# The head of a decoder layer: activation tiles and the first weight chunk taken token tile by token tile

## The chip, the cores and the metric

One core of one Trainium2 chip. TensorE (PE) multiplies, VectorE (DVE) and ScalarE (ACT) do the elementwise work, GpSimd (POOL) a few small operations, and SyncE (SP) issues the loads. The metric is the device time of one execution in microseconds (us). Before the change it is 766.53 us, the median of three runs (766.51 to 766.59).

## The reference, cut to what matters

```python
mod = silu(c) @ w_mod + b_mod                       # c: (1, 1024), w_mod: (1024, 6*1024)
sh_m, sc_m, gt_m, sh_f, sc_f, gt_f = split(mod, 6)
h = rms_norm(x, g_mix_norm) * (1.0 + sc_m) + sh_m    # x: (512, 1024)
proj = h @ w_in                                      # (512, 5704): queries, keys, values, gates
...                                                  # two sparse attentions, gates, w_out
x = x + gt_m * (merged @ w_out)
h = rms_norm(x, g_ffn_norm) * (1.0 + sc_f) + sh_f
x = x + gt_f * ((silu(h @ w_gate) * (h @ w_up)) @ w_down)
```

Everything is float32. The change touches only the first two hundred instructions or so: the normalization of x, the part of the modulation that it needs, and the first 128 of the 1024 rows of `w_in`.

## The kernel before, in words

**Tiles.** Tokens come in four tiles of 128 (`NT`), features in eight chunks of 128 (`NK`). x is loaded as four token tiles into two buffers `xa` (tag O); an x tile is 512 KB. A matmul needs features on partitions, so each x tile is transposed block by block on TensorE (`turn`, a product with `identr`) after it was scaled by 1/rms. The transposed x is kept in `xnT` (tag O): two buffers of four chunks each.

**Scale of a token.** For tile i: ACT squares it and sums the row (`V<-O` in the profile), DVE adds EPS (`m<-ssx`), POOL raises to -0.5 (`m<-m,mhalf`), DVE multiplies the tile (`O<-O,m`).

**Modulation of a chunk.** For chunk k the kernel needs the 128 scales and 128 shifts of its features: a product of silu(c) with a strip of `w_mod` (tag K, two loads of 512 KB: m=1 for the scale, m=0 for the shift). It sums eight blocks j per half: ACT does the first two (`first_products`, `gu<-K,cs`), DVE adds some of the others (`add_up`, `gu<-K,cs,gu`, then `gu<-gu`), and for chunks 0 and 1 TensorE takes the blocks named in `direct` (`pstr<-cs,K`). A product with a column of ones (`pstr<-one,gu`) sums DVE's part over the partitions. The two columns that come out are called `pc`. From them come the columns `acol` and `mcol`, and the normalized chunk is `x*acol+mcol`.

**High and low parts.** A float32 product is made of three fast ones: each operand is split into a rounded high part and the rest. For the activations these are `hh` and `hl` (tag H; `s` holds the unrounded chunk, and DVE subtracts, `H<-s,H`), for the weights `wh` (an ACT cast of the loaded `st`) and `wl` (a DVE subtraction, `wl<-st,wh`).

**The first group.** `first_group(k, ...)` multiplies chunk k's four token tiles with 512 columns of keys (banks `acc_k`, tag psacc) and three of them with 512 columns of index queries (banks `acc_q` in the banks pspv, pss, pstr): seven outputs, three products each, 21 matmuls. In the middle of group k-1 stands `between`, the `pc` products of chunk k. The loop over k runs `add_up(k+1)`, group k-1 with chunk k's `pc`, then `shift_scale(k)` (`acol`, `mcol` on ACT), `high`, `s`, `low`, and the weights of chunk k+1.

**Order.** Each engine runs its own instructions in the order in which the code issues them; the head is written out by hand. Behind the head a planner in the kernel places small tasks between the matmuls by costs of its own. PSUM has four banks psacc, two pstr, one pspv, one pss. `unused_products` are matmuls whose result nobody reads. All loads of the head go through SP's queue, in order; before they are x 0 to 3, strip 0, first weights 0, strip 1, first weights 1.

Instructions of PE, DVE, ACT and POOL go through a recording wrapper, so the profile gives them all the wrapper's line, L111; they are told apart by their tiles.

Of the kernel before, what the change touches and what calls it, by code (L numbers as in the profile page):

```python
# [23 lines left out]
F32 = mybir.dt.float32  # L24
# [93 lines left out]
def layer(ctx, tc, x, vecs, w_mod, w_in, gvecs, w_br_dsa, w_br_moba, w_out, w_gate_up, w_down, cosh, sinh, cosi, sini, out):  # L118
# [102 lines left out]
    for i in range(NT):  # L221
        nc.sync.dma_start(xa[i // 2][:, i % 2, :], xv[:, i, :])
    strips = [load_strip(0)]
    firsts = [load_first(0)]
    strips.append(load_strip(1))
    firsts.append(load_first(1))

# [31 lines left out]
    def first_group(k, wh, wl, between):  # L259
# [4 lines left out]
        def high_high(n0, n1):  # L264
            for acc, i, ws in outs[n0:n1]:
                te.matmul(acc, hh[:, sls[i]], wh[:, 0, ws], start=k == 0, stop=False)
# [9 lines left out]
        if not k:  # L276

            high_high(0, 4)
            high_low(0, 4)
            high_high(4, 7)  # L280
            low_high(0, 4)
            high_low(4, 7)
            between()
            low_high(4, 7)
            return
# [7 lines left out]
    with tc.manual_schedule(engines=engines):  # L293
# [16 lines left out]
        direct = {(0, 1): (5, 6, 7), (0, 0): (5, 6, 7), (1, 1): (6, 7), (1, 0): (6, 7)}  # L310
# [51 lines left out]
        def turn(i, ks):  # L362
            for k in ks:
                te.transpose(xps[k][:, i * P:(i + 1) * P], xa[i // 2][:, i % 2, k * P:(k + 1) * P], ident)

        def unused_products(n, where=None):

            where = bank[:, 1:] if where is None else where[:, P:]
            for _ in range(n):
                te.matmul(where, identr, identr.unsqueeze(1).to_broadcast([P, 3, P]), start=True, stop=True)  # L370

        def keep(k, eng):
            eng(xnT[k // 4][:, k % 4, :], xps[k])


        xps = [ps(g) for g in ["tr", "pv", "s"] + ["acc"] * 4]
        bank = ps("tr", (P, 4, P))
        pc = bank[:, 0, 0:2]
        ws = []
        xs = [xa[i // 2][:, i % 2, :] for i in range(NT)]  # L380
        rs = [small([P, 1]) for _ in range(NT)]

# [3 lines left out]
        def rstd(i, more):  # L386
            ve.tensor_scalar(rs[i], ssx[:, i:i + 1], more, None, op0=ALU.add)
            ge.tensor_tensor(out=rs[i], in0=rs[i], in1=mhalf[:, 0:1], op=ALU.pow)

        unused_products(14)  # L390
        for i in range(NT - 1):
            se.activation(junk, xs[i], AF.Square, scale=D ** -0.5, accum_out=ssx[:, i:i + 1])
            rstd(i, EPS)
            if i < NT - 2:
# [47 lines left out]
        for k in range(1, NK):  # L442
# [6 lines left out]
            if k == 1:  # L449
                first_products(2)  # L450
# [1520 lines left out]
```

## Time and profile before

| | |
|---|---|
| median of three runs | 766.53 us (766.51 to 766.59) |
| span of the profiled execution | 764.9 us; what lies around it, against the median, is 1.6 us |
| TensorE | busy 756.1 us, 99% of the span |
| VectorE, ScalarE, GpSimd | busy 603.4, 413.6 and 62.1 us |
| granted TensorE clock | 1.000 over the span |
| loads and stores | 137.10 MB, 179 GB/s on average |

The profile page gives the span, not a time of its own for the profiled execution; so the span is set against the median. Rows of the timeline give start and duration in us, the engine, what is written and read, how many instructions were merged (x4), and in brackets an idle time before them with what ended it. PE's matmuls overlap: the step from one start to the next, not the duration, is what one costs in a row.

### The profile page before, as it was taken

The numbers are of one execution on the slowest core, as the hardware profiler recorded it, in microseconds if no ns is written. First come the engines' busy times: TensorE is split into PE (matmuls) and PEld (weight loads), VectorE is DVE, ScalarE is ACT, GpSimd is POOL, SyncE is SP. The second block draws the span as 40 slices with busy tenths as digits, with TensorE's granted clock in tenths as the row PEclk, the third lists the DMA queues.
The fourth block names the chain that finished last, engine by engine and source line by source line (L and its number), as shares of the span: only waits on it lengthen the run. The fifth ranks groups of instructions, "written<-read, shape, count | busy, mean of one in ns | idle before, by whom it ended". The sixth has DMA issues, their size and how long they took to land.

```text
span 764.9 us, 10986 instructions
## 1 busy us (share of the span) xinstructions
PE 756.1 (99%) x3884; PEld 639.2 (84%) x3884; DVE 603.4 (79%) x1183; ACT 413.6 (54%) x888; POOL 62.1 (8%) x91
## 2 busy tenths in 40 slices
PE   7999999999999999999999999999999999999998
PEld 6887888888788887888888988889999998888886
DVE  6974889989799796336867897878788856997897
ACT  6763786879868666643534443543444432554431
POOL 2000012011111000000000000000011020012100
PEclk9999999999999999999999999999999999999999
DMA  9976252542125455533440146744565679589982
GB/s 324 353 212 227 85 169 81 159 129 59 40 79 198 134 147 179 175 98 131 143 152 1 56 150 205 243 153 133 182 204 186 198 254 377 185 264 390 311 324 82
DMA packets 87921, 137.10 MB, mean 179 GB/s; under 512 B 9008, under 2 KB 49272, under 8 KB 87228
## 3 DMA queue, kind: packets, MB, share of 16 engines
q1 hardware_dynamic: 79992, 105.71, 43.5%
q0 software_dynamic: 7792, 30.67, 11.2%
q8 instruction: 30, 0.49, 0.3%
q14 instruction: 23, 0.19, 0.1%
q10 hardware_dynamic: 84, 0.04, 0.0%
HBM read 117.52 MB, written 18.88 MB: 178 GB/s over the span
## 4 chain that ended last, share of the span: by engine, by line
PE 97%; DVE 1%; ACT 0%; DMA 0%; issue 0%; POOL 0%; ACTq 0%
PE psacc L111 62%; PE pstr L111 12%; PE pspv L111 11%; PE pss L111 11%; DVE V L111 1%; DVE s L111 1%; DMA pT<-in_vecs_dram 0%; POOL m L111 0%; DVE O L111 0%; ACT H L111 0%; ACT V L111 0%; DVE m L111 0%; ACT acol L111 0%; DVE cols L111 0%; DVE mcol L111 0%
## 5 line engine op out<-in xcount | busy, mean ns | idle before, releaser
L111 DVE TENSOR_TENSOR wl<-st,wh 128x1024 fp32r<-128x1024 f32 (+1 forms) x98 | 113.7, 1160 | 42.3 <-ACT wh L111 32.9
L111 PE MATMUL psacc<-wh,H 128*128 128x512 f32 x384 | 126.4, 400 | 0.5 <-ACT H L111 0.5
L111 ACT CAST wh<-st 128x1024 fp32r<-128x1024 f32 (+1 forms) x98 | 97.7, 999 | 53.2 <-DMA st<-in_w_gate_up_dram 20.7
L111 PE MATMUL psacc<-H,wh 128*128 128x512 f32 x384 | 124.1, 404 | 0.0
L111 PEld LDWEIGHTS psacc<-wh,H 128*128 128x128 f32 x384 | 72.0, 188 | 16.0 <-ACT H L111 1.1
L111 PEld LDWEIGHTS psacc<-H,wh 128*128 128x128 f32 x384 | 70.0, 188 | 15.3 <-issue 2.7
L111 PE MATMUL psacc<-H,wl 128*128 128x512 f32 x192 | 75.1, 391 | 0.0
L111 PE MATMUL psacc<-H,O 128*128 128x256 f32 (+1 forms) x465 | 72.3, 296 | 0.0
L111 PE MATMUL psacc<-wl,H 128*128 128x512 f32 x192 | 71.0, 390 | 0.0
L111 PEld LDWEIGHTS psacc<-H,O 128*128 128x128 f32 x465 | 64.0, 191 | 2.7
L111 POOL TENSOR_TENSOR m<-m,mhalf 128x4 f32<-128x4 f32 (+1 forms) x24 | 28.6, 1192 | 390.1 <-DVE m L111 356.1
L111 PE MATMUL psacc<-K,O 128*128 128x256 f32 x288 | 43.4, 283 | 0.0
L111 PEld LDWEIGHTS psacc<-H,wl 128*128 128x128 f32 x192 | 36.0, 188 | 8.0
L111 PEld LDWEIGHTS psacc<-wl,H 128*128 128x128 f32 x192 | 36.2, 188 | 6.8
L111 PE MATMUL pss<-H,wh 128*128 128x512 f32 x128 | 39.5, 390 | 0.0
L111 PE MATMUL pspv<-H,wh 128*128 128x512 f32 x128 | 39.4, 389 | 0.0
L111 PE MATMUL psacc<-O,wh 128*128 128x512 f32 x128 | 39.4, 389 | 0.0
L111 PEld LDWEIGHTS psacc<-K,O 128*128 128x128 f32 x288 | 38.4, 191 | 0.0
L111 ACT ACTIVATE s<-s,att 128x256 f32<-128x256 f32 (+3 forms) x64 | 34.2, 562 | 4.5 <-DVE att L111 4.3
L111 ACT CAST H<-st 128x512 fp32r<-128x512 f32 (+1 forms) x21 | 16.1, 766 | 23.4 <-PE psacc L111 18.4
L111 ACT CAST O<-pT 128x512 fp32r<-128x512 f32 x24 | 14.7, 621 | 25.7 <-DVE pT L111 25.2
L111 PEld LDWEIGHTS pspv<-H,wh 128*128 128x128 f32 x128 | 24.0, 188 | 5.0
(338 smaller groups left out, 1629.5 us busy)
## 6 DMA issues: line engine op xcount, KB each, us to landing
st<-in_w_in_dram SPq DMA_DIRECT2D x36, 512.0 KB, 3.5
K<-in_w_mod_dram SPq DMA_DIRECT2D x12, 1024.0 KB, 6.5
st<-in_w_gate_up_dram SPq DMA_DIRECT2D x24, 512.0 KB, 4.1
st<-in_w_down_dram SPq DMA_DIRECT2D x22, 512.0 KB, 4.9
st<-in_w_gate_up_dram SPq DMA_DIRECT2D x40, 256.0 KB, 3.6
K<-in_w_mod_dram SPq DMA_DIRECT2D x16, 512.0 KB, 6.3
O<-second POOLq DMA_DIRECT2D x6, 768.0 KB, 8.0
st<-in_w_in_dram SPq DMA_DIRECT2D x16, 256.0 KB, 4.2
```

Of the source, the lines that this page charges most:

```text
L111: inst = f(*args, **kw)
```

## The change

**Loads.** The first strip goes between the x tiles 1 and 2, and the two halves of the first weights go behind x 2 and x 3. Strips and first weights up to strip 3 are issued right behind them; before, they came later in the code but in the same place of SP's queue. On SP before (K is a strip, O an x tile, st first weights):

```order
L222 DMA O_74<-in_x_dram 128x1024 x2
L222 DMA O_75<-in_x_dram 128x1024 x2
L213 DMA K_80<-in_w_mod_dram 128x8x128 x2
L184 DMA st_83<-in_w_in_dram 128x512 x2
L213 DMA K_86<-in_w_mod_dram 128x8x128 x2
L184 DMA st_89<-in_w_in_dram 128x512 x2
```

and now:

```order
L223 DMA O_74<-in_x_dram 128x1024 x2
L213 DMA K_78<-in_w_mod_dram 128x8x128 x2
L223 DMA O_75<-in_x_dram 128x1024
L230 DMA st_first<-in_w_in_dram 128x512
L223 DMA O_75<-in_x_dram 128x1024
L232 DMA st_first<-in_w_in_dram 128x512
L213 DMA K_86<-in_w_mod_dram 128x8x128 x2
L184 DMA st_89<-in_w_in_dram 128x512 x2
```

From K_86 on the queue is as it was; the second pair of x tiles (O_75) moved behind the strip.

**Transposes.** An x tile's eight blocks go into two banks of the tile's own, four chunks each, rather than into one bank per chunk; each bank is then copied to `xnT` by one instruction. Before, chunk 7 was transposed later, inside the loop; now all eight are done in the head.

**Chunk 0, tile by tile.** `first_group` no longer handles chunk 0. Its `pc` is made after x tiles 0 and 1, its products run for tiles 0 and 1 before tiles 2 and 3 are scaled and transposed, and the `pc` of chunk 1 stands among the last of them. TensorE before, from chunk 0's `pc` to the middle of its group:

```order
L111 MATMUL pstr_137<-one,gu_208 128x1
L111 MATMUL pstr_137<-cs,K_80 128x1 x3
L111 MATMUL pstr_137<-one,gu_208 128x1
L111 MATMUL psacc_133<-identr 128x384 x5
L111 MATMUL psacc_249<-wh_218,H_104 128x512
```

and now, from the same place to the transposes of tile 3 and the first query products:

```order
L111 MATMUL psacc_220<-wh_213,H_113 128x512
L111 MATMUL psacc_221<-wh_213,H_113 128x512
L111 MATMUL psacc_220<-wl_214,H_113 128x512
L111 MATMUL psacc_221<-wl_214,H_113 128x512
L111 MATMUL pspv_234<-identr,O_75 128x128 x4
L111 MATMUL pss_239<-identr,O_75 128x128 x4
L111 MATMUL psacc_220<-wh_213,H_115 128x512
L111 MATMUL psacc_221<-wh_213,H_115 128x512
L111 MATMUL psacc_222<-wh_213,H_113 128x512
L111 MATMUL psacc_222<-wl_214,H_113 128x512
L111 MATMUL pstr_254<-identr,O_75 128x128 x4
L111 MATMUL pstr_259<-identr,O_75 128x128 x4
```

Sixteen transposes (those of x tiles 2 and 3, O_75) moved from before chunk 0's products to between them.

**VectorE.** The scaling of x tiles 2 and 3 moved behind chunk 0's columns. Now, from these columns to the low part of the last two tiles:

```order
L111 TENSOR_SCALAR mcol<-pstr_139,cols 128x1
L111 TENSOR_SCALAR H_113<-O_137,acol,mcol 128x256
L111 TENSOR_SCALAR m_1_23_142<-ssx 128x1
L111 TENSOR_TENSOR wl_214<-st_first,wh_213 128x512
L111 TENSOR_SCALAR O_75<-O_75,m_1_23_142 128x1024
L111 TENSOR_SCALAR s_219<-O_137,acol,mcol 128x256
L111 TENSOR_TENSOR H_115<-s_219,H_113 128x256
L111 TENSOR_SCALAR m_1_24_143<-ssx 128x1
L111 TENSOR_SCALAR O_75<-O_75,m_1_24_143 128x1024
```

Both scalings (the rows O_75<-O_75) had been done before the sums of chunk 0. The sums of chunk 2 moved too. Before, with gu_256 and gu_283 the sums of chunks 1 and 2, and H_106 the low part of chunk 1:

```order
L111 TENSOR_TENSOR gu_256<-gu_256 128x256
L111 TENSOR_TENSOR wl_265<-st_89,wh_264 128x1024
L111 SCALAR_TENSOR_TENSOR gu_283<-K_268,cs,gu_283 128x256 x6
L111 TENSOR_TENSOR gu_283<-gu_283 128x256
L111 TENSOR_TENSOR H_106<-s_328,H_104 128x512
```

and now, with gu_283 and gu_319 the sums of chunks 1 and 2, and H_115 the low part of chunk 1:

```order
L111 TENSOR_TENSOR gu_283<-gu_283 128x256
L111 TENSOR_TENSOR wl_303<-st_89,wh_302 128x1024
L111 TENSOR_TENSOR H_115<-s_314,H_113 128x512
L111 SCALAR_TENSOR_TENSOR gu_319<-K_92,cs,gu_319 128x256 x6
L111 TENSOR_TENSOR gu_319<-gu_319 128x256
```

The low part of chunk 1 now stands ahead of the sums of chunk 2. From the weights of chunk 2 on, the order on every engine is what it was.

The diff, cut:

```diff
-    for i in range(NT):
-        nc.sync.dma_start(...)
...
+    load_x(0)
+    load_x(1)
     strips = [load_strip(0)]
-    firsts = [load_first(0)]
+    load_x(2)
+    firsts = [wp.tile([P, 1, 512 + N_Q], F32, name="st_first", tag="st")]
+    nc.sync.dma_start(firsts[0][:, 0, 0:512], w_in[0:P, C_KB:C_KB + 512])
+    load_x(3)
+    nc.sync.dma_start(firsts[0][:, 0, 512:512 + N_Q], w_in[0:P, C_QI:C_QI + N_Q])
...
-        direct = {(0, 1): (5, 6, 7), (0, 0): (5, 6, 7), (1, 1): (6, 7), (1, 0): (6, 7)}
+        direct = {(0, 1): (4, 5, 6, 7), (0, 0): (4, 5, 6, 7), (1, 1): (6, 7), (1, 0): (6, 7)}
...
-        unused_products(14)
+        unused_products(10)
...
+        turn(0, ("pv", "s"))
+        unused_products(1)
+        first_products(0, 1)
+        scale(1)
+        keep(0, 0, se.copy)
+        sum_direct(0, pc, 1)
+        add_up(0, 1)
+        turn(1, ("tr", "acc"))
...
+        sum_up(0, pc, (0,), begun=True)
+        keep(0, 1, se.copy)
+        keep(1, 0, ve.tensor_copy)
+        unused_products(3)
+        square(2)
...
+        scale(2)
+        low_tokens(slice(0, 256))
+        rstd(3)
+        turn(2, ("pv", "s"))
...
+        high_tokens(3)
+        keep(2, 1, se.copy)
...
             if k == 1:
-                first_products(2)
-            if k + 1 < NK:
-                add_up(k + 1)
...
+                first_products(2)
+                add_up(2)
             if k + 1 < NK:
                 next(weights_hi(k + 1))
                 weights_lo(k + 1)
```

In the new code `unused_products` writes into `bank`, the PSUM tile that also holds chunk 0's `pc`; before, the five products behind that `pc` wrote into another bank. The squares of x tiles 2 and 3 are both done whole by ACT (before, DVE took half of the last one).

More of the change, by code (lines that the diff above doesn't have):

```diff
@@ L360, in weights_lo, with turned, keep, unused_products @@
                              op=ALU.subtract)
[L362 to L368, printed above, removed]
+        def turned(i, half, tag):
+            to = ps(tag, (P, 4, P))
+            for q in range(4):
+                k = half * 4 + q
+                te.transpose(to[:, q, :], xa[i // 2][:, i % 2, k * P:(k + 1) * P], ident)
+            return to
+        def keep(i, half, eng):
+            eng(xnT[half][:, :, i * P:(i + 1) * P], turns[i][half])
+        def unused_products(n):
             for _ in range(n):
[L370 to L376, printed above, removed]
+                te.matmul(bank[:, 1:], identr, identr.unsqueeze(1).to_broadcast([P, 3, P]), start=True, stop=True)
         bank = ps("tr", (P, 4, P))
@@ new lines, in product, with shifted, low_tokens @@
+        def product(i, to, part, act, weight, first=False, last=False):
+            te.matmul(to[i], act[:, sls[i]], ws[0][weight][:, 0, part], start=first, stop=last)
+        def shifted(to, src):
+            ve.tensor_scalar(to, src, acol[:, 0, 0:1], mcol[:, 0:1], op0=ALU.mult, op1=ALU.add)
+        def low_tokens(c):
+            shifted(hf0[:, c], xnT[0][:, 0, c])
+            ve.tensor_tensor(out=hl0[:, c], in0=hf0[:, c], in1=hh0[:, c].bitcast(F32), op=ALU.subtract)
+        hh0, hl0 = hk(0)
@@ L420, in layer @@
         ve.tensor_scalar(mcol[:, 0:1], pc[:, 0:1], bm[:, 0:1], None, op0=ALU.add)
+        parts = weights_hi(0, (KB, QI))
         next(parts)
[L422 to L431 removed]
@@ new lines, in layer, with high_tokens @@
+        rstd(3)
+        turn(2, ("pv", "s"))
+        next(parts)
+        for i in range(2):
+            product(i, acc_k, KB, hl0, 0)
+        def high_tokens(i):
+            se.activation(hh0[:, sls[i]], turns[i][0][:, 0, :], AF.Identity, bias=mcol[:, 0:1], scale=acol[:, 0, 0:1])
+        high_tokens(2)
+        keep(2, 0, se.copy)
+        scale(3)
+        product(2, acc_k, KB, hh0, 0, first=True)
+        product(2, acc_k, KB, hh0, 1)
+        keep(1, 1, se.copy)
+        weights_lo(0, QI)
@@ L465, in layer @@
             if k == 1:
-                keep(NK - 1, se.copy)
+                first_products(2)
+                add_up(2)
             if k + 1 < NK:
```

126 lines of the change are left out of this document (67 added, 59 removed).

## The prediction, before the changed kernel was run

> **What bounds the kernel now.** I read first what TensorE waited for over the whole span, then the busy time in four stretches.
>
> ```profile
> PE pstr L111 <- DMA pT<-in_vecs_dram: 4.0, 1, 4.0
> PE pstr L111 <- DVE O L111: 0.5, 1, 0.5
> PE psacc L111 <- ACT H L111: 0.5, 2, 0.3
> ...
> 0.00:15.71 15.71, 10.82 (x69) 9.97 (x69) 8.71 (x28) 9.88 (x20) 4.66 (x12) 1.00 0.91 316
> 15.71:22.76 7.05, 6.86 (x37) 5.62 (x37) 6.98 (x15) 5.41 (x12) 0.00 (x0) 1.00 1.12 363
> 22.76:28.20 5.44, 5.44 (x25) 4.50 (x26) 5.09 (x12) 4.60 (x9) 0.00 (x0) 1.00 1.12 358
> 28.20:764.90 736.70, 732.94 (x3755) 619.10 (x3753) 582.62 (x1133) 393.65 (x850) 57.42 (x79) 1.00 0.53 173
> ```
>
> The first three rows (waiter, what ended the wait, us in all, times, longest) are all the waits that TensorE has, and they lie in the head. In the stretches the columns behind the length are busy time of PE, weight loads, DVE, ACT and POOL. Chunk 0's products begin at 15.71, group 1 at 22.76, group 2 at 28.20, and from there PE works without a wait. So the order behind the head being the same, a shift of group 2's start should reach the end whole, and nothing downstream can take it up. In 15.71:22.76 VectorE is busy 6.98 of 7.05 us: the head is full on two engines, and that is where the change adds and moves work.
>
> TensorE's rows there:
>
> ```profile
> 4.14 3.96 PE L111 MATMUL pstr<-identr 128*128 128x384 f32 x14
> ...
> 11.35 0.60 PE L111 MATMUL psacc<-identr,O 128*128 128x128 f32 x4
> 11.79 0.73 PE L111 MATMUL pstr<-cs,K 128*128 128x1 f32 x6
> 12.38 0.64 PE L111 MATMUL psacc<-identr,O 128*128 128x128 f32 x4
> ...
> 14.26 1.13 PE L111 MATMUL psacc<-identr 128*128 128x384 f32 x5
> 15.71 1.19 PE L111 MATMUL psacc<-wh,H 128*128 128x512 f32 x4 [0.32 <-ACT H L111]
> 16.74 1.08 PE L111 MATMUL psacc<-wl,H 128*128 128x512 f32 x4
> 17.66 0.39 PE L111 MATMUL pspv<-wh,H 128*128 128x512 f32 x1
> ...
> 22.76 1.21 PE L111 MATMUL psacc<-wh,H 128*128 128x512 f32 x4 [0.19 <-ACT H L111]
> ...
> 25.66 0.50 PE L111 MATMUL pstr<-one,gu 128*128 128x1 f32 x4
> ...
> 28.20 1.07 PE L111 MATMUL psacc<-wh,H 128*128 128x512 f32 x4
> ```
>
> Steps from them: a transpose 0.11 (four from 11.35 to 11.79), a direct strip product 0.20 (three, recorded as six, from 11.79 to 12.38), a product of 512 columns 0.23 (four from 16.74 to 17.66), an unused one about 0.2. The product with ones is taken at 0.2 like a direct one.
>
> VectorE's, ScalarE's and GpSimd's:
>
> ```profile
> 6.82 0.75 DVE L111 TENSOR_SCALAR O<-O,m 128x1024 f32<-128x1024 f32 x1 [0.68 <-POOL m L111]
> 8.30 0.76 DVE L111 TENSOR_SCALAR O<-O,m 128x1024 f32<-128x1024 f32 x1 [0.67 <-POOL m L111]
> ...
> 14.57 0.21 DVE L111 TENSOR_SCALAR mcol<-pstr,cols 128x1 f32<-128x1 f32 x1
> 15.30 0.68 DVE L111 TENSOR_TENSOR wl<-st,wh 128x512 fp32r<-128x512 f32 x1
> 15.90 0.80 DVE L111 TENSOR_SCALAR s<-pstr,acol,mcol 128x512 f32<-128x512 f32 x1
> 21.13 2.46 DVE L111 SCALAR_TENSOR_TENSOR gu<-K,cs,gu 128x256 f32<-128x256 f32 x6
> 23.62 0.42 DVE L111 TENSOR_TENSOR gu<-gu 128x256 f32<-128x256 f32 x1
> 23.97 0.68 DVE L111 TENSOR_TENSOR H<-s,H 128x512 fp32r<-128x512 f32 x1
> ```
>
> ```profile
> 16.02 0.60 ACT L111 COPY O<-pspv 128x512 f32<-128x512 f32 x1
> 21.36 0.35 ACT L111 ACTIVATE acol<-pstr,bmg,cols 128x1 f32<-128x1 f32 x1 [0.21 <-PE pstr L111]
> 21.89 0.81 ACT L111 ACTIVATE H<-O,mcol,acol 128x512 fp32r<-128x512 f32 x1
> 22.62 0.80 ACT L111 ACTIVATE s<-O,mcol,acol 128x512 f32<-128x512 f32 x1
> ...
> 6.22 0.56 POOL L111 TENSOR_TENSOR m<-m,mhalf 128x1 f32<-128x1 f32 x1 [3.75 <-DVE m L111]
> 9.20 1.75 POOL L111 TENSOR_TENSOR m<-m,mhalf 128x1 f32<-128x1 f32 x2 [0.93 <-DVE m L111]
> ```
>
> POOL's power took 0.56 us once and 0.88 each (1.75 for two) later; I carry both.
>
> **The loads.** Issue and landing of x 0, x 3 and the first strip half before:
>
> ```profile
> L222 SPq DMA_DIRECT2D O<-in_x_dram x1: 392/392/392, 0.7 to 0.7; - x1
> DMA to landing us min/median/max: 4.0/4.0/4.0
> ...
> L222 SPq DMA_DIRECT2D O<-in_x_dram x1: 432/432/432, 2.1 to 2.1; - x1
> DMA to landing us min/median/max: 6.3/6.3/6.3
> ...
> L213 SPq DMA_DIRECT2D K<-in_w_mod_dram x1: 577/577/577, 2.6 to 2.6; - x1
> DMA to landing us min/median/max: 7.4/7.4/7.4
> ```
>
> x 0 lands at 4.7, x 3 at 8.4, the strip's first half at 10.0: 1.25 us for an x tile, 1.55 for a strip half, one behind the other. In the new order the strip halves land at 4.7+1.25+1.55 = 7.5 and 9.05, x 2 at 10.3, the first half of the weights by 11.0 (256 KB, half of a 512 KB load at most), x 3 by 12.3, the second half by 13.1. Everything behind them has the same bytes ahead of it and lands as before. SP's issue moves nobody else: nothing waits on SP but its loads.
>
> **Up to the first product: a gain of 2.5 us.** x 0 and x 1 arrive and are scaled as before, by 7.57 and 9.06. Ten unused products rather than fourteen leave PE free before 7.57. Then PE runs in one piece: eight transposes 0.88, an unused one 0.26, four direct 0.8, eight transposes 0.88, ones 0.2, four direct 0.8, ones 0.2, three unused 0.6: from 7.63 to 12.2. DVE's two sums of the first half are over by 10.3 even at the price of 256 columns (9.06 + 3 x 0.42), before PE asks at 10.45. The columns wait for the third unused product, since these write into the tile that holds `pc`: its result is there 0.15 us behind its step, 12.35; before, they did not wait for unused ones, so this costs 0.7. Then `acol` and `mcol` 0.35, the high part of 256 tokens 0.42 (an estimate between `mcol` 0.21 and 512 columns 0.80), and the first product starts at 13.2, against 15.71.
>
> **From there to chunk 1's `pc`: the gain is lost.** Before, this stretch had 21 products and four direct ones; now 16 transposes (1.76) are in it, and DVE's chain. From 13.15 in DVE's order: m, weights' low part 0.6, beside it POOL's power 0.56 to 0.88 (to 13.9 to 14.3), scaling of x 2 0.75 (to 14.8), s and low part of tiles 0 and 1 0.8 (15.6), m 0.15, power 0.6 (16.3), scaling of x 3 0.75 (17.1). PE waits for both scalings: about 0.3 and 0.5. Behind the second stand four transposes and their result 0.65 (17.8), ACT's high part of tile 3 0.46 (an estimate, between `acol` 0.35 and 0.81), ACT's copy of tile 2's second bank 0.6 (its bank is the next product's): 18.85, where PE waits again 0.5 behind its pspv product. From there PE has ten products 2.3 + 0.1 for the restart, two direct 0.4, two products 0.45 + 0.1, ones 0.2, direct 0.4, ones 0.36: `pc` of chunk 1 is there at 23.1. ACT and DVE have its sums ready by about 22, just in time. Before, `acol` started behind it at 21.36: 1.7 us earlier.
>
> **From `pc` to group 2: 1.8 us more.** Group 1 starts 1.2 behind `pc` (`acol` to high part 0.53 as from 21.36 to 21.89, half a high part 0.58, an estimate by the same two rows, and hand-overs): 24.3, against 22.76, 1.5 late. Now the moved sums of chunk 2 decide. DVE holds them behind the low part of chunk 1, and that needs the whole `s`: second half of the high part 0.5, `s` 0.8, so DVE starts 2.4 behind `pc`, at 25.5; low part 0.6, six sums 2.5 (21.13 to 23.62), the last 0.42: 29.0. PE reaches its ones of chunk 2 2.9 behind group 1's start (22.76 to 25.66), at 27.2, and waits 1.8 us. Before, these sums were over when PE came. DVE meanwhile stands idle before the low part, with strip 2 loaded. From the ones to group 2 it is 2.54 (25.66 to 28.20): 29.0 + 2.54 = 31.55, against 28.20: 3.3 us late. Later groups have DVE's work of 5.1 in a step of 5.3 and the same order, so no wait is added and none removed.
>
> Sum: -2.5 to the first product, +4.0 to group 1 (transposes 1.76 less the four before at 22, 0.44; waits 1.3; restarts 0.3; at the end chunk 1's `pc` stands last, with nothing of 1.3 us left to do beside its columns), +1.8 in group 1. 764.9 + 3.3 = 768.2 of span; with the 1.6 around it, and so against the median, 769.8 us.
>
> Bounds: with POOL at 0.56 and the estimates at their low rows 0.5 less; with every restart and change between transposes and products at 0.1 (the first of 1.19 against 1.08) 0.5 more. Without PE's waits for scalings and copies 1.3 less, and without the one in group 1 another 1.8.
>
> [...] The unused products at the start of the head, before 6.9 and after:
>
> ```profile
> L111 PE MATMUL pstr<-identr x9: 379/522/667, 4.1 to 6.8; 128*128 128x384 f32 x9
> ...
> L111 PE MATMUL pstr<-identr x7: 334/337/522, 6.5 to 7.8; 128*128 128x384 f32 x7
> ```
>
> They get faster, 522 to 337 ns, about 2.9 us after PE began. The new kernel's ten reach to 7.2, so the same activity comes before that moment, and I take full speed from there. [...]
>
> **The rivals.**
> Not slower: DVE's chain isn't what PE waits for, because the sums and scalings are done earlier than I place them. Place: the scalings of x 2 and x 3, and the ones of chunk 2; price 1.3 + 1.8 = 3.1, time 766.7. It decides the sign from where these waits together stay under 1.5. For it: by my own sum DVE has over 2 us idle before chunk 1's low part, so it has the time. Against: the order puts the work behind that wait, and DVE's stretch was 99% busy before.
> Only half: group 1's wait for chunk 2's sums is not there: 3.3 - 1.8 = 1.5, 768.0.
> [...]
> Faster: the first product's 2.5 us reach the end: 764.0. PE's own 21 products, 16 transposes and `pc` need 7.9 us behind 13.2 even with no wait, so `pc` would still come at 21.1; only a far earlier first product gives it.
>
> **How the numbers follow.** My forecast, slower by 2.0 to 4.2: 0.74. Cold: 0.06. Only half: 0.10, half of it under the 0.2% (1.5 us) that a measurement can tell. Not slower 0.06, faster 0.04. So slower 0.85, same 0.11, faster 0.04. Range 768.0 to 771.2: what lies outside is the not slower and faster cases, most of the cold one and some of the half one, 0.2.
>
> **What would show it.** Right: first product near 13.2; PE waiting for DVE's O and ACT's O between 14 and 19; DVE idle over 2 us before the H<-s,H of chunk 1; PE waiting near 1.8 us for DVE gu at the ones of chunk 2; no PE wait behind it. Wrong: group 2 starting before 29.7, or transposes at a step of over 0.15 behind 7.6.

## The result, and the profile after

The changed kernel takes 771.0 us, the median of five runs (770.78 to 772.84), against 766.53 us for the kernel before in the same comparison (766.50 to 766.70, five runs). The ratio is 1.0062 with a 95% interval of 1.0050 to 1.0074: slower by 4.5 us. The forecast was slower by 3.3 us, 769.8. Its bounds do not agree: 2.0 to 4.2 us slower in one place, 768.0 to 771.2 us, which is 1.5 to 4.7 slower, in another; the median lies outside the first and inside the second. The sign came, and so did the waits. The sum was 1.2 us short, because it takes a full TensorE clock throughout.

The profiled execution is the slowest of the five: span 771.1 us, time 772.84, mean granted clock 0.996. The other four have spans of 769.0 to 769.3 us at a mean clock of 0.998. Before, the clock is 0.999 to 1.000 in every run.

What TensorE waited for up to 40 us, after the change (us in all, times, longest):

```profile
PE pstr L111 <- DMA pT<-in_vecs_dram: 3.7, 1, 3.7
PE pstr L111 <- DVE gu L111: 1.7, 1, 1.7
PE psacc L111 <- ACT H L111: 1.2, 1, 1.2
PE psacc L111 <- DVE m L111: 1.0, 1, 1.0
PE pspv L111 <- DVE O L111: 0.4, 1, 0.4
PE pss L111 <- ACT O L111: 0.4, 1, 0.4
PE pspv L111 <- DVE m L111: 0.2, 1, 0.2
```

The first stood there before too, and the last, ahead of the first transposes, is small. The others are waits that the prediction has: chunk 2's sums (1.8 foreseen, 1.7), the shift of chunk 1 behind a `pc` that now stands last (1.2), the columns ahead of the first product (0.98 of idle time in the row at 13.40 below), the scaling of tile 2 and a copy. Only the wait for the scaling of tile 3 is missing: it was done at 17.37, and PE came to these transposes at 18.29.

The same four stretches as before the change, cut at the first product, group 1 and group 2 (PE, PEld, DVE, ACT, POOL busy, then the granted clock):

```profile
0.00:13.40 13.40, 8.51 (x51) 7.74 (x52) 6.02 (x22) 8.58 (x16) 2.91 (x11) 1.00 0.88 308
13.40:25.43 12.03, 10.06 (x50) 7.91 (x50) 8.11 (x16) 6.73 (x16) 1.47 (x2) 0.86 1.11 357
25.43:33.98 8.55, 6.86 (x25) 5.18 (x26) 7.31 (x16) 6.80 (x13) 0.00 (x0) 0.85 1.11 352
33.98:771.10 737.12, 733.35 (x3755) 619.40 (x3753) 581.88 (x1131) 392.58 (x848) 57.45 (x79) 1.00 0.52 170
```

Before they were 15.71, 7.05, 5.44 and 736.70 us, all at 1.00. The two middle ones now have 0.86 and 0.85 in the clock column. Cut finer, at the places where the granted clock changes, which lie on a grid of 3.413 us (the stretches at one clock from the first rise on are 6.83, 3.41, 13.65 and 3.41 us long):

```profile
7.54:10.95 3.41, 3.38 (x31) 3.39 (x31) 2.67 (x9) 2.50 (x7) 0.56 (x1) 1.00 1.08 402
10.95:14.37 3.42, 2.44 (x15) 1.75 (x14) 1.77 (x7) 3.22 (x6) 0.93 (x1) 1.00 1.09 362
14.37:17.78 3.41, 3.03 (x12) 2.43 (x11) 2.71 (x6) 1.41 (x4) 0.55 (x1) 0.50 1.08 355
17.78:21.19 3.41, 3.06 (x18) 2.34 (x17) 1.90 (x5) 2.29 (x7) 0.00 (x0) 1.00 1.11 363
...
28.02:31.43 3.41, 1.72 (x10) 1.16 (x9) 3.38 (x8) 1.66 (x6) 0.00 (x0) 1.00 1.08 355
31.43:34.85 3.42, 3.42 (x10) 2.64 (x9) 3.39 (x9) 3.20 (x5) 0.00 (x0) 0.50 1.07 341
```

The column knows the clock from its first rise on, 7.54 us here, and reads 1.00 ahead of it, though the ten unused products up to there take 0.36 us each and the three at 11.65 about 0.2. Two whole stretches of 3.41 us are at half clock, each behind a stretch in which TensorE was busy for 2.44 and 1.72 us only. TensorE's rows there (start, duration, idle time in front):

```profile
13.40 0.71 PE L111 MATMUL psacc<-wh,H 128*128 128x512 f32 x2 [0.98 <-DVE m L111]
...
15.26 1.09 PE L111 MATMUL pspv<-identr,O 128*128 128x128 f32 x4 [0.38 <-DVE O L111]
16.14 1.06 PE L111 MATMUL pss<-identr,O 128*128 128x128 f32 x4
...
18.29 1.03 PE L111 MATMUL pstr<-identr,O 128*128 128x128 f32 x8
...
25.43 1.23 PE L111 MATMUL psacc<-wh,H 128*128 128x512 f32 x4 [1.23 <-ACT H L111]
...
30.18 0.61 PE L111 MATMUL pstr<-one,gu 128*128 128x1 f32 x4 [1.69 <-DVE gu L111]
...
31.20 1.71 PE L111 MATMUL psacc<-wh,H 128*128 128x512 f32 x4
...
33.98 1.49 PE L111 MATMUL psacc<-wh,H 128*128 128x512 f32 x4
```

Four transposes take a step of 0.88 at 15.26 (0.22 each); the eight at 18.29 run at the 0.1 that the sum used. The seven products from 31.20 to 33.98 take 2.78 us, 0.40 each instead of 0.23: 1.2 us lost in one place.

VectorE ahead of chunk 2's ones is as foreseen, idle for 2.41 us in front of chunk 1's low part, with the moved sums behind it:

```profile
26.61 0.69 DVE L111 TENSOR_TENSOR H<-s,H 128x512 fp32r<-128x512 f32 x1 [2.41 <-ACT s L111]
27.21 2.46 DVE L111 SCALAR_TENSOR_TENSOR gu<-K,cs,gu 128x256 f32<-128x256 f32 x6
29.71 0.42 DVE L111 TENSOR_TENSOR gu<-gu 128x256 f32<-128x256 f32 x1
```

So the first theory is: the waits are what was predicted, and the rest is the half clock which they let in. The rival is a sum that was short elsewhere. In the tests that follow the kernel before was run along each time, with medians of 766.5 to 766.6 us.

| run | median, us | lowest and highest | ratio, 95% interval | granted clock of the runs |
|---|---|---|---|---|
| the changed kernel | 771.0 | 770.78, 772.84 | 1.0050 to 1.0074 | 0.996 to 0.998 |
| 1 fill | 771.7 | 770.80, 771.82 | 1.0050 to 1.0074 | 0.997 to 0.999 |
| 2 sums early | 771.43 | 770.38, 772.62 | 1.0050 to 1.0074 | 0.993 to 0.998 |
| 3 own bank | 770.76 | 769.74, 772.59 | 1.0042 to 1.0068 | 0.994 to 0.998 |
| 4 loads only | 773.72 | 770.36, 773.86 | 1.0066 to 1.0093 | 0.993 to 1.000 |
| 5 warm | 771.55 | 770.49, 771.89 | 1.0044 to 1.0071 | 0.997 to 1.000 |
| 6 rstd early | 772.49 | 769.73, 772.82 | 1.0056 to 1.0083 | 0.993 to 0.998 |
| 7 old loads | 774.94 | 774.21, 776.60 | 1.0097 to 1.0124 | 0.991 to 0.996 |
| 8 warm, sums, rstd | 767.95 | 767.87, 769.55 | 1.0013 to 1.0031 | 0.998 to 1.000 |
| 9 reordered | 767.79 | 766.62, 769.02 | 1.0003 to 1.0021 | 0.998 to 1.000 |
| 10 one column | 769.73 | 769.50, 771.36 | 1.0028 to 1.0053 | 0.997 to 0.998 |
| 11 reordered, old loads | 768.2 | 768.00, 768.71 | 1.0009 to 1.0027 | 0.999 to 1.000 |
| 12 before, less unused | 766.63 | 766.41, 769.25 | 0.9995 to 1.0013 | 0.994 to 1.000 |
| 13 rstd(2) back | 766.97 | 766.64, 769.28 | 1.0000 to 1.0018 | 0.999 to 1.000 |
| 14 scaled on VectorE | 766.82 | 766.62, 767.30 | 0.9995 to 1.0013 | 0.999 to 1.000 |

One run of the fourth kernel (949 us) and one of the fourteenth (2709 us) were disturbed; the table leaves them out.

### The profile page after: what moved, and what is told of

Read it like the earlier page. It is cut to its first block, busy times and chain, and to the rows that moved or that the text cites. A ratio compares the mean times of both kernels' runs of the same rounds, so it can differ in the third digit from the quotient of the medians.

```text
span 771.1 us, 10984 instructions
## 1 busy us (share of the span) xinstructions
PE 758.8 (98%) x3879; PEld 640.2 (83%) x3879; DVE 603.3 (78%) x1183; ACT 414.7 (54%) x890; POOL 61.8 (8%) x91
## 4 chain that ended last, share of the span: by engine, by line
PE 96%; DVE 2%; DMA 1%; issue 0%; ACT 0%; POOL 0%; SPq 0%; DVEq 0%
PE psacc L111 61%; PE pstr L111 12%; PE pspv L111 11%; PE pss L111 11%; DMA K<-in_w_mod_dram 1%; DVE s L111 1%; DVE V L111 1%; DMA O<-in_x_dram 1%; DVE gu L111 0%; DVE O L111 0%; POOL m L111 0%; ACT V L111 0%; SPq L184 0%; DVE m L111 0%; ACT H L111 0%
## 5 line engine op out<-in xcount | busy, mean ns | idle before, releaser
L111 PE MATMUL psacc<-wh,H 128*128 128x512 f32 x384 | 128.5, 405 | 2.2 <-ACT H L111 1.2
L111 PEld LDWEIGHTS psacc<-O,wh 128*128 128x128 f32 x128 | 24.0, 188 | 5.0
## 6 DMA issues: line engine op xcount, KB each, us to landing
O<-second POOLq DMA_DIRECT2D x6, 768.0 KB, 7.6
```

Of the source, the lines that this page charges most:

```text
L111: inst = f(*args, **kw)
```

## The experiments

**What lowers the clock? Runs 1, 5, 10 and 12.** Run 1 puts unused products into three of the waits:

```diff
+        unused_products(5, acc_k[0]...)      # ahead of the first product
+            if k == 2: unused_products(8, pc2[:, 1:])   # ahead of chunk 2's ones
+            if k == 1: unused_products(3, pc1[:, 1:])   # ahead of group 1
```

> The changed kernel with unused products put into three of TensorE's waits (5 ahead of the first product, 3 behind chunk 1's shift, 8 ahead of the ones of chunk 2); no order of other work changes. Theory (the sum of 3.3 us was right and the rest of the 4.5 is half clock that TensorE gets after a 3.4 us window with about 1 us or more of waiting): no stretch of half clock behind the head's start, mean clock 1.000, group 2 starts near 31.7, time 769.0 to 769.8, so 1.2 to 2 us under the changed kernel's 771.0. Rival (the 4.5 us are waits alone, the clock costs nothing): 770.8 to 771.3, as before the edit. Rival (unused products stand in the way of real ones): 771.5 or more.

Measured: 771.7, no better; it lies where the expectation puts products that stand in the way, but the clock was not full either. The three waits were filled all but 0.3 us of the last and 0.6 for chunk 1's shift, and yet one half-clock stretch stayed:

```profile
9.92:13.33 3.41, 3.41 (x30) 3.41 (x31) 1.49 (x4) 3.21 (x8) 0.00 (x0) 1.00 1.07 388
13.33:16.74 3.41, 3.41 (x11) 2.88 (x10) 2.55 (x8) 0.51 (x2) 0.93 (x1) 0.50 1.11 369
```

The stretch in front of it is 3.41 of 3.41 us busy. So idle time alone is not it. What that stretch holds are eight transposes, 18 records of one-column products (the direct blocks and the ones) and three unused products: many instructions, few columns. The second half stretch, in group 1, went away with the eight fillers.

The profiles of runs 1, 2, 3 and 6 differ from the changed kernel's at the start too. Up to the transposes of tile 0 they have its order on TensorE, and yet their clock first rose at 9.92, 9.71, 9.44 and 9.69 us instead of 7.54. The first transposes and the first product of run 2, where nothing ahead of them was edited:

```profile
7.60 1.12 PE L111 MATMUL pspv<-identr,O 128*128 128x128 f32 x4
8.51 1.06 PE L111 MATMUL pss<-identr,O 128*128 128x128 f32 x4
...
14.59 1.19 PE L111 MATMUL psacc<-wh,H 128*128 128x512 f32 x2 [0.98 <-DVE m L111]
```

and the same transposes of the changed kernel:

```profile
7.57 0.66 PE L111 MATMUL pspv<-identr,O 128*128 128x128 f32 x4 [0.25 <-DVE m L111]
8.06 0.60 PE L111 MATMUL pss<-identr,O 128*128 128x128 f32 x4
```

Four of them take 0.91 us in the one and 0.49 in the other, and the first product comes at 14.59 instead of 13.40. So between these two profiles the late rise costs 1.2 us, and the mean granted clock of a run does not show it. Whether the four unprofiled runs of the changed kernel had one is not known. The rise came at another place in each profile, by the grid: in all traces it stands behind a window in which TensorE was busy for 2.88 us or more (before, 3.51 to 6.92), and not behind 2.82 or less (run 5, 1.32 to 4.74).

Run 5 begins the unused products earlier and puts some among the one-column products too, at the same order of all else:

```diff
+        for _ in range(6): te.matmul(spare[:, 1:], identr, ...)   # ahead of the turn of vecs' rows
-        unused_products(1)
+        unused_products(3, spare[:, 1:])      # behind the turn of tile 0
+        unused_products(2, spare[:, 1:])      # behind the turn of tile 1
-        unused_products(3)
+        unused_products(4, spare[:, 1:])      # behind chunk 0's sums; 8 and 4 in group 1 as in run 1
```

> Leaves out nothing; adds unused 384-column products on TensorE: six ahead of the turn of the rows of vecs (TensorE stands there until 4.0 us anyway), two more behind the turn of tile 0, two behind the turn of tile 1, four instead of three behind chunk 0's sums, and, as in the run with fills before, four behind chunk 1's pc and eight ahead of the ones of chunk 2; order of all else as in the changed kernel. Theory 'clock': what the sum lacks is the half clock, so that with an array kept busy from 2 us on the clock is full from some 5 to 8.5 us and stays full; the first product of chunk 0 then stands at 13.0 to 13.8, group 2 at 31.2 to 32.0 us, that is 3.0 to 3.8 behind before's 28.20, and the time is 769.5 to 770.3 us. Rival 'the sum was short elsewhere': the clock is full and the time is 770.8 us or more with group 2 at 32.6 or later. Rival 'one-column products count as idle': a half-clock stretch stays behind the products of chunk 0's pc, and time and clock are as in the changed kernel (770.8 to 772.8).

Measured: 771.55 in the median, but two of the five runs have a full clock (1.000 and 0.999) and take 770.49 and 770.66; the other three, at 0.997, take 771.55 to 771.89. The profiled one shows what is left, in group 1's approach:

```profile
21.81:25.22 3.41, 2.81 (x20) 2.52 (x20) 1.90 (x3) 1.42 (x4) 0.00 (x0) 1.00 1.11 325
25.22:28.63 3.41, 3.41 (x10) 2.63 (x9) 2.49 (x6) 3.41 (x7) 0.00 (x0) 0.50 1.06 333
```

The clock theory's 769.5 to 770.3 was missed narrowly even by the runs at full clock. The theory neither stands nor falls with this run alone.

From the first eight traces and the two kernels' own a count came out that parts the windows. Take each stretch of 3.413 us at full clock on the grid, and add up the columns that its products stream: 512 or 384 for these, 256 for a transpose (its step of 0.11 us for 128 columns is half of the 0.23 for 512), nothing for a product of one column. A product that a window's edge cuts is divided at 2.4 columns a ns, the rate of the fullest windows (some 8200 in 3.413 us). Run 10 was made to test it. It is run 8 (below; clock full in eight of eleven runs), in which fifteen of the unused products were given one column instead of 384, at the same places:

```diff
-                te.matmul(where, identr, identr.unsqueeze(1).to_broadcast([P, 3, P]), start=True, stop=True)
+                te.matmul(where[:, 0, 0:1], ident, one, start=True, stop=True)
```

> Leaves out nothing. The kernel of the eighth run, with the fifteen unused products behind the first turn (three, two, four, four and two of 384 columns) made unused products of one column, as many and at the same places; the first sixteen stay as they are. Theory 'columns': the array issues instructions for nearly as long, but streams 5760 columns less; windows of the pc's then hold 0.28 to 0.39 of the columns, half-clock stretches of 3.413 us come back, and the time is 769.0 to 771.5 us with a mean clock of 0.993 to 0.998. Rival 'idle time': what lowers the clock is that TensorE has nothing to issue; the clock stays full, and the time is 767.6 to 768.1, 0.0 to 0.3 less than in the eighth run, since the products are shorter.

Measured: 769.73, every run at 0.997 or 0.998, 1.8 us above run 8. Of run 10:

```profile
9.79:13.20 3.41, 3.41 (x33) 3.41 (x33) 2.07 (x9) 2.87 (x5) 0.55 (x1) 1.00 1.06 390
13.20:16.61 3.41, 3.41 (x13) 2.92 (x13) 3.38 (x8) 0.78 (x3) 0.65 (x1) 0.50 1.12 369
```

and of run 8 at about the same place:

```profile
8.35:11.76 3.41, 3.41 (x31) 3.41 (x30) 3.02 (x9) 3.06 (x7) 0.00 (x0) 1.00 1.04 412
11.76:15.17 3.41, 3.22 (x19) 2.28 (x19) 2.58 (x8) 1.91 (x4) 1.01 (x2) 1.00 1.13 353
```

Both first lines are busy to the full and hold 33 and 31 records; 2048 columns are in the one, some 4300 in the other. The clock falls behind the one and not the other. Idle time, the rival, is out: it would have given 767.6 to 768.1.

Over all 16 traces, 13 of over 3400 full-clock windows are followed by half clock:

| window from, us | columns | clock of the next window |
|---|---|---|
| run 10, 9.79 | 2048 | half |
| changed kernel, 28.02 | 2207 | half |
| changed kernel, 10.95 | 2829 | half |
| run 1, 9.92 | 3078 | half |
| run 3, 23.09 | 3172, the most of all that fell | half |
| run 10, 6.37 | 3297, the fewest of all that stayed | full |
| run 12, 10.94 | 3415 | full |
| changed kernel, 21.19 | 3542 | full |
| before, 10.33 | 3584 | full |

By this count the parting holds without an exception, at some 3200 columns, two fifths of what the fullest windows stream (some 8200). How the edges are cut matters: by the starts of products alone a window that fell has 3584 columns and one that stayed 2944, so the limit is known no better than to a product. The weights 256 and 0 were chosen on ten of the traces; the six later ones agree, but only run 10 has a fall among them.

Idle time fails from the other side too. In run 4 (below) TensorE was busy for less of this window than of any that fell, with a wait of 2.40 us across its end, and the next window reads 1.00 again; the count gives it some 3300 columns:

```profile
10.25:13.66 3.41, 1.68 (x13) 1.32 (x11) 1.12 (x5) 2.17 (x6) 0.55 (x1) 1.00 1.07 381
```

The grid lies differently in each profile (the clock rises at 6.92, 7.54, 9.92, 8.15 and so on), so, by this count, any stretch of 3.4 us of this head with fewer than some 3200 columns can be the one that falls. Run 12 asks whether the kernel before owes its steady clock to its unused products, and takes nine of them out:

```diff
-                unused_products(2)
-        unused_products(5, xps[3])
```

> Leaves out nothing of the result. The kernel before without nine of its unused products (two behind each of the turns of tiles 0 and 1, and the five ahead of chunk 0's group); its first fourteen stay. Theory 'columns': the stretch of 3.413 us from 11.5 to 16 us then has windows with 0.22 to 0.38 of the columns (0.44 and more with them), so that in most runs half clock falls on the first group: 767.0 to 769.0 us, mean clock 0.995 to 0.999, spread between runs over 0.5 us. Rival 'idle time does not matter below a window': the gaps are at most 1.4 us, the clock stays full, 766.3 to 767.2.

Measured: eight of the eleven runs stay at 766.41 to 766.80, three fall to 0.994 to 0.998 and take 768.10 to 769.25. The median is that of before, so the size was overrated: "most runs" was wrong. But falls there are now, presumably by the phase of the grid (no trace of these three was kept), and none shows in the runs of before (0.999 or 1.000 in all; one of them took 768.36 us all the same).

**Are the waits worth what the sum says? Runs 2, 3, 6 and 8.** Run 2 moves `first_products(2)` and `add_up(2)` ahead of `shift_scale(1)`, where chunk 2's sums stood before the change:

```diff
         weights_lo(1)
+        first_products(2)
+        add_up(2)
...
-            if k == 1:
-                first_products(2)
-                add_up(2)
```

> The changed kernel with the sums of chunk 2 issued ahead of chunk 1's columns and low part, as they stood before the change. Theory: TensorE's 1.7 us wait at the ones of chunk 2 is gone and nothing takes its place, 1.8 us less, and if the half-clock stretch came from this wait up to 1.7 more: 767.5 to 769.4. Rival (the wait only moves to the low part of chunk 1, which DVE then does later): 770.5 to 771.2.

Measured: 771.43, so nothing was won in the median. Yet the wait of 1.7 us is not in its list of waits any more, and from group 1 (27.06) to group 2 (33.89) it takes 6.83 us instead of 8.55. What the edit gave went into the late rise of the clock and into half clock from 13.12 to 19.95 and from 26.77 to 30.18, three windows.

Run 3 lets the three unused products ahead of the first product write to `acc_k[0]` instead of the tile that holds `pc`.

> The changed kernel with the three unused products behind chunk 0's sums written into another bank, so that the columns do not wait for them. Theory: the first product starts 0.5 to 0.7 us earlier (12.8 rather than 13.4) and the whole head behind it with it: 770.3 to 770.6 at the same clock, down to 768.8 if the shorter wait also saves a half-clock stretch. Rival (DVE or the loads hold the next step anyway): 770.9 to 771.1.

Measured: 770.76, lowest 769.74; first product at 13.67, not at 12.8, and 0.994 of clock in the profile. The time decides nothing. The clock rose late here too (9.44), and against run 2, where it did so at 9.71, the first product is 0.9 us earlier: that speaks for the theory's 0.5 to 0.7.

Run 6 makes the powers of tiles 2 and 3 early:

```diff
         square(2)
+        rstd(2)
...
         scale(2)
+        rstd(3)
         low_tokens(slice(0, 256))
-        rstd(3)
```

> Leaves out nothing; moves VectorE's and GpSimd's rstd(2) ahead of acol, and rstd(3) right behind the scaling of tile 2, so that the power of tiles 2 and 3 isn't waited for. Theory 'chain': the waits of 0.3 and 0.5 us of the turns of tiles 2 and 3 for the scalings go, group 1 and group 2 come 0.6 to 0.8 us earlier at the same clock, and the median is 770.0 to 770.4. Rival 'the clock takes it': the stretches at half clock stand at other places and take 0 to 1.7 us more or less; the median lies between 769.5 and 771.5 without a sign. Rival 'not on the path': VectorE waits for square(2) ahead of acol, and nothing is won, 770.8 to 771.2.

Measured: 772.49, *more* than the changed kernel, with four runs at 0.993 to 0.996. In the one with 0.998 it is 769.73, 1.1 to 1.3 below the changed kernel's runs at 0.998 (770.78 to 771.06), where the chain promised 0.6 to 0.8. The profiled one:

```profile
9.69:13.10 3.41, 3.41 (x31) 3.41 (x31) 1.88 (x6) 2.54 (x6) 0.55 (x1) 1.00 1.05 391
13.11:16.52 3.41, 2.43 (x7) 1.49 (x7) 2.77 (x8) 1.51 (x3) 0.64 (x1) 0.50 1.11 365
16.52:19.93 3.41, 3.41 (x14) 2.92 (x13) 1.39 (x3) 1.42 (x3) 0.01 (x1) 0.50 1.12 347
```

So one by one these edits measure the clock and not the edit. Run 8 does the two together with run 5's unused products (two ahead of chunk 2's ones):

> Leaves out nothing; e5's unused products (two instead of eight ahead of the ones of chunk 2), with the moved sums of chunk 2 ahead of the scalings of chunk 1 (as in the second run) and rstd(2), rstd(3) early (as in e6). Theory 'clock and chain': with a full clock the wait of 1.7 us ahead of chunk 2's ones and the 0.6 to 0.8 us of the powers are won together: group 2 at 29.0 to 29.9 us and 767.0 to 768.2 us, that is still 0.5 to 1.7 above before. Rival 'the clock takes it': a half-clock stretch stays in the head; 768.8 us or more.

Measured: 767.95; eight of eleven runs lie within 767.87 to 768.08 at 0.999 or 1.000, three at 0.998 take 769.4 to 769.6. Groups 1 and 2:

```profile
23.86 1.10 PE L111 MATMUL psacc<-wh,H 128*128 128x512 f32 x4
...
29.49 1.07 PE L111 MATMUL psacc<-wh,H 128*128 128x512 f32 x4
```

At a full clock the two edits are worth about 2.6 us (770.5 to 770.7 in run 5, 767.9 here; the six unused products that run 8 has fewer stand in run 5 in the wait for chunk 2's sums): the prediction's waits for scalings and for chunk 2's sums are 0.3 + 0.5 + 1.8 = 2.6. And one half stretch, which is what 0.998 stands for, is worth about 1.5 us (769.4 to 769.6 against 767.9).

**What is the order of the loads worth? Runs 4, 7 and 11.** Run 4 is the kernel before with the new order of the loads only.

> The kernel before with the new order of loads alone. Theory: this order needs the tile by tile order of the work; without it the scalings of x 2 and x 3 stand ahead of the sums on DVE and x 3 lands 3.8 us later, so the first product comes at 18.7 to 19.5 rather than 15.7: 769.3 to 770.3, and 1 to 2 more if the longer wait brings half clock. Rival (the first product hangs on the strip, not on x): 766.0 to 766.8.

Measured: 770.36 at a full clock, 772.3 to 773.9 at 0.993 to 0.998. Of the run at full clock:

```profile
14.33 0.33 PE L111 MATMUL pstr<-identr,O 128*128 128x128 f32 x1 [2.40 <-DVE O L111]
...
19.44 0.73 PE L111 MATMUL psacc<-wh,H 128*128 128x512 f32 x2 [0.33 <-ACT H L111]
```

The old head needs all four x tiles ahead of its first product, which stands at 19.44 instead of 15.71: 3.7 us later, as is the time.

Run 7 is the changed kernel with the loads of before.

> Leaves out nothing; the changed kernel with the loads in the order of before (four x tiles, strip 0, first weights, strip 1, and so on). Theory 'chain': the halves of strip 0 land some 2 us later (9.6 and 10.5 us by before's rows), the sums of chunk 0 and all behind them start 1.4 to 1.8 us later, and the time is 772.2 to 773.0. Rival 'x tiles bound it': the turns of tiles 2 and 3 come earlier by the 1.3 us that x2 and x3 land earlier and the time is that of the changed kernel or less, 769.5 to 771.0.

Measured: 774.94, 3.9 above the changed kernel where the chain alone has 1.6; clock 0.991 to 0.996, with half clock from 11.05 to 21.29 and from 34.95 to 38.36 in the profile. So this run does not price the loads alone. Run 11 repeats the question on the reordered head of run 9, with unused products in the wait for strip 0:

> Leaves out nothing. The kernel of this call's first run with the loads in the order of before, and ten instead of two unused products behind the first turn and three more behind, which fill the wait for strip 0. Theory 'chain': at a full clock the later strip 0 alone moves all behind it by 1.5 to 2.1 us: group 2 at 29.0 to 30.0 us, time 1.4 to 2.1 above the first run of this call, so 767.4 to 768.5. Rival 'x tiles': x2 and x3, which land 1.3 us earlier, give it back; within 0.5 us of the first run.

Measured: 768.2 with all runs at 0.999 or 1.000; 0.4 above run 9 in the median, which is the rival's, and 1.4 between the lowest runs, which is the chain's. The profile is on the chain's side, but gives less than its 1.5 at the end:

```profile
15.24 0.70 PE L111 MATMUL psacc<-wh,H 128*128 128x512 f32 x2 [0.17 <-DVE H L111]
...
24.63 1.23 PE L111 MATMUL psacc<-wh,H 128*128 128x512 f32 x4
...
30.08 1.07 PE L111 MATMUL psacc<-wh,H 128*128 128x512 f32 x4
```

Its first product is 1.79 us behind run 9's, its group 1 1.53, its group 2 1.07. So the loads alone cost 3.7 us, and the tiles with the old loads 0.4 (run 11, in the median) to 3.9 us (run 7, much of it the clock) more than with the new: neither part stands well without the other.

**Can the order be made to pay? Runs 9, 13 and 14.** Run 9 takes the waits out and keeps 3600 columns and more in every window by the program's order:

```diff
-        direct = {(0, 1): (4, 5, 6, 7), (0, 0): (4, 5, 6, 7), ...
+        direct = {(0, 1): (5, 6, 7), (0, 0): (5, 6, 7), ...
+        rstd(2)                       # ahead of acol; rstd(3) right behind scale(2)
+        first_products(1, 1)          # chunk 1's half m=1 behind scale(3)
+        add_up(1, 1)                  # and ahead of the turn of tile 3
+        sum_up(1, pc, (1,), begun=True)
+        sum_up(1, pc, (0,))           # chunk 1's pc ahead of the last four products
+        first_products(2)             # chunk 2's sums ahead of shift_scale(1)
+        add_up(2)                     # and unused products: 6, 12, 2, 1, 1, 4, 2
```

> Leaves out nothing. The head by token tiles with its waits taken out: rstd(2) and rstd(3) early; three instead of four direct blocks in chunk 0; chunk 1's scaled blocks and sums of the half m=1 ahead of the copies of tiles 1 to 3; chunk 1's pc ahead of the last four products of chunk 0, so that the shift is computed behind them; chunk 2's sums ahead of the scalings of chunk 1; unused 384-column products from 2 us on and in the waits. Theory 'columns': TensorE is set to half clock for 3.413 us behind a window of 3.413 us in which it streamed less than some 0.40 of the columns that it can at full clock (a transpose counted as 256, a one-column product as nothing); here no window has less than 0.44 by the program's order, so that the clock is full from 5 to 9 us on in every run; and the chain gives group 1 at 22.2 to 22.7 and group 2 at 27.4 to 28.0 us against before's 22.76 and 28.20, so 765.9 to 766.5 us with little spread. Rival 'clock again': a half stretch stays in some of the runs, 767 us or more in these. Rival 'strip 2': chunk 2's sums end later than group 1's products (they landed at 20.8 us in the changed kernel), group 2 stands at 28.5 or later, 767 us or more at a full clock.

Measured: 767.79, from 766.62 to 769.02; the forecast of 765.9 to 766.5 with little spread was missed. Nine of the eleven runs are at 0.999 or 1.000, the slowest (769.02, at 1.000) among them, so most of the spread is not the clock's. The other two are at 0.998, where the count expected none; no trace of them was kept. The profile has the first product at 13.45, group 1 at 23.10 and group 2 at 29.01 instead of 27.4 to 28.0, the first two behind operations that wait for a load ahead of the columns:

```profile
12.44 0.15 DVE L111 TENSOR_SCALAR m<-ssx 128x1 f32<-128x1 f32 x1 [0.60 <-ACT V L111]
12.51 0.21 DVE L111 SCALAR_TENSOR_TENSOR acol<-pstr,cols,bmg 128x1 f32<-128x1 f32 x1
```

```profile
21.12 0.91 ACT L111 ACTIVATE gu<-K,cs 128x256 f32<-128x256 f32 x2 [0.89 <-DMA K<-in_w_mod_dram]
21.93 0.34 ACT L111 ACTIVATE acol<-pstr,bmg,cols 128x1 f32<-128x1 f32 x1
```

Here x 2 landed at 11.18 us and strip 2 at 21.03; in run 8 at 10.27 and 20.12. Runs 13 and 14 take the two away, `rstd(2)` back behind the shift of tiles 0 and 1, then also the scaled blocks of strip 2 to VectorE:

```diff
-        first_products(2)
+        first_products(2, on_dve=True)    # ve.tensor_scalar(dst(j), src(j), cs[:, j:j + 1], None, op0=ALU.mult)
```

> Leaves out nothing. The reordered head (e9) with rstd(2) put back behind the shift of tiles 0 and 1, so that VectorE's acol does not stand behind the squares of x 2. Theory 'landing': the first product stands at 12.7 to 13.5 whenever x 2 lands; ScalarE's scaled blocks of strip 2, ahead of chunk 1's acol, still wait where strip 2 lands late, so some of the spread stays: lowest run 766.4 to 766.8, highest 767.5 to 768.5. Rival 'not the head': the same spread as in e9 (766.6 to 769.0) about the same median.

> Leaves out nothing. As e13, and the first two scaled blocks of strip 2 are made by VectorE rather than ScalarE, so that nothing stands ahead of chunk 1's acol that waits for a load; VectorE has 0.95 us more to do ahead of chunk 2's sum. Theory 'landing': the spread shrinks to under 1 us, group 1 stands at 22.4 to 23.0, group 2 at 27.9 to 28.7 by where strip 2 lands, and the median is 766.3 to 767.0, the same as before within 0.1%. Rival 'VectorE pays': chunk 2's ones wait more than 0.5 us for its sums, 767.0 or more. Rival 'not the head': the spread of e9.

Measured: 766.97 (nine of eleven runs up to 767.32, two at 768.3 and 769.3), then 766.82 with all ten within 766.62 to 767.30. Of run 14:

```profile
12.83 0.70 PE L111 MATMUL psacc<-wh,H 128*128 128x512 f32 x2 [0.16 <-DVE m L111]
...
22.82 1.21 PE L111 MATMUL psacc<-wh,H 128*128 128x512 f32 x4
...
28.25 1.07 PE L111 MATMUL psacc<-wh,H 128*128 128x512 f32 x4
```

Group 2 stands at 28.25, before's at 28.20: the time is that of before (0.9995 to 1.0013). "Landing" met all its numbers in run 14, and missed the highest run in run 13 (767.5 to 768.5 expected). It fits, but it is not shown: the spread is 2.4 us in run 9, 2.6 in run 13 (0.7 but for two runs) and 0.7 in run 14, the landings in the two runs above 768 us are not on record, and the kernel before, run along, spread from 766.46 to 768.36 beside run 9 and only from 766.42 to 766.88 beside runs 13 and 14. No version beats the kernel before; a head by tiles can be brought level with it.

## Why the prediction was right or wrong

| step | predicted | profiled | of it, at half clock |
|---|---|---|---|
| strip 0's halves, x 2 landed | 7.5 and 9.05, 10.3 | second half 8.99, x 2 10.78 | |
| first product | 13.2 | 13.40 | |
| first product to group 1 | 11.1 | 12.03 | 14.37 to 17.78 |
| wait for chunk 2's sums | 1.8 | 1.69 | |
| group 1 to group 2 | 7.25 | 8.55 | 31.43 to 33.98 |
| behind group 2 | 736.7 | 737.12 | 33.98 to 34.85 |
| span | 768.2 | 771.1; the four others 769.0 to 769.3 | |

**Right: the waits.** The gain of 2.5 us at the first product came (2.3). It was lost where the sum loses it: 16 transposes in the stretch, the waits for scaling and copy (0.38 and 0.35), `pc` last, then 1.7 us for chunk 2's sums, with VectorE idle for 2.41 us just before. Nothing behind group 2 took it up. Runs 5 and 8, both at full clock, confirm the price of the scalings and of chunk 2's sums (2.6 us).

**Wrong: "I take full speed from there".** This is the step that failed: half clock behind the rise is a term that the sum has at nothing, and the only reason given concerns the rise itself. The granted clock was 0.86 and 0.85 in the two stretches that the sum is about, and the prediction's own mark against it, a transpose step of over 0.15 us behind 7.6, is in the rows at 15.26 (0.22). The profiled run is over the forecast by 0.93 between first product and group 1, by 1.30 in group 1 and by 0.42 behind, together 2.65 of the 2.9 us that the span lies above the forecast, and each of these stretches holds half clock. The rows price it: the seven products from 31.20 lose 1.2 us, the eight transposes from 15.26 lose 0.7. A half stretch of 3.413 us lowers a mean clock over 770 us by 0.002, so the four runs at 0.998 have had about one; at the 1.5 us that one costs in run 8, their 769.0 to 769.3 would be 767.5 to 767.8 at a full clock, 0.4 to 0.7 below the predicted span of 768.2. That is a reckoning: no run of the changed kernel itself had a full clock, and a late rise, which the mean does not show, would put it lower still. The nearest is run 5, whose span, with products added on the path, is 768.7 to 768.9 at a full clock. From both sides the rest of the sum was right within about 0.7, by what is known, and the miss is the clock.

Of the chances only the 0.06 for "cold" went to a clock that is not full in the first stretch. In the profile of the changed kernel it rose at 7.54, in time. But in runs 1, 2, 3 and 6 it rose late, at 9.44 to 9.92, and in run 2 that cost 1.2 us. So the chance was too small, and the step to full speed, that the products come before the moment at which the clock rose, took one trace's moment for a fixed one: even with fourteen products at the start it was 6.92 (before), 7.52 (run 12) and 10.25 us (run 4). What the working failed to do besides was to ask of *each* later stretch whether the change leaves enough in it. The material stood in the profile of before: its products ahead of group 0 that nobody reads, and a PE column that is nowhere below 2.88 of 3.41 us.

In the traces every stretch at one clock, from the first rise on, is a multiple of 3.413 us long, with another place of the grid in each profile. The length of a gap did not tell where the clock falls: the longest gap ahead of a fall was 1.69 us in the changed kernel, in runs 1 and 10 there was none, and behind the 2.40 us of run 4 the clock stayed full. Transposes have to be counted: a window of before from 10.33 has fourteen of them and next to nothing else of more than one column, and the next one stays full.

**The loads** behind x 2 do not all land "as before": x 2 came between 10.10 and 11.33 us in the profiles with the new order, and strip 2 came 0.91 us later in run 9 than in run 8 (21.03 against 20.12), as x 2 did (11.18 against 10.27). In the changed kernel this cost nothing that the trace shows, since chunk 2's sums start by VectorE's order and not by the landing; in run 9 it did.

## What to carry to other kernels

Where a granted clock moves as it did here, count for every stretch of its grid (3.413 us in these traces) how many columns TensorE streams, before and after the edit. One-column products and a wait of 0.98 us together left 2829 columns in a window of the changed kernel, and the next one ran at half clock. Products that nobody reads may be what holds it: with fifteen of them cut to one column, all five runs of run 10 were at 0.997 or 0.998, where run 8 has 0.999 or 1.000 in eight of eleven. Where the clock moves, single edits cannot be told apart by their times (runs 1, 2, 3 and 6: medians of 770.76 to 772.49 us against 771.0): keep it full first, then measure. A mean granted clock says nothing of a late first rise, since the column reads 1.00 ahead of it; the steps of the first transposes do (0.91 us for four in run 2, 0.49 in the changed kernel). An operation that waits for a load belongs behind, not ahead of, the short operations on the path in its engine's queue, for landings moved by up to 1.2 us from profile to profile (x 2 from 10.10 to 11.33).

## What the runs showed of the hardware that was not expected

- By the count above, the granted clock fell to half behind windows of 3.413 us with at most 3172 columns streamed (13 windows), never behind 3297 or more (over 3400 windows). Windows busy for 3.41 of 3.41 us fell too, when most of their instructions were products of one column (run 1 from 9.92, 18 of 30 records; run 10 from 9.79, 2048 columns in 33 records).
- The first rise came between 4.93 (run 8) and 10.25 us (run 4), behind a window busy for 2.88 of 3.41 us or more. With one and the same start of the head it was 7.54 in the changed kernel's profile and 9.44 to 9.92 in those of runs 1, 2, 3 and 6.
- Half-clock stretches last one window or several: 3.41, 6.83 and 10.24 us were seen (the changed kernel, run 2, run 7). The grid's place differs from profile to profile, and the clock and the time of one and the same kernel from run to run: 767.9 at 0.999 or 1.000 and 769.5 at 0.998 in run 8, 766.5 at 1.000 and 768.1 or more at 0.994 to 0.998 in run 12. That the grid's place makes this difference was not shown.
- With a strip ahead of it, the third x tile landed between 10.10 and 11.33 us in the profiles, 1.2 to 2.3 us behind the strip in front of it, and in run 9 strip 2 landed later than in run 8 by the same 0.91 us as x 2. What sets it is open.
